# Attention values in two wide blocks with seven products, kept in the queries' place; row sums made for two pairs at a time, and early for the down products

## The chip, the core and the metric

The kernel runs on one core of a Trainium2 chip. The metric is the device time of one execution in microseconds. Each engine of the core has its own instruction stream: TensorE (PE in the profile; its weight loads are PEld) multiplies matrices into PSUM, VectorE (DVE) and ScalarE (ACT) compute elementwise, GpSimd (POOL) does little here, and SyncE (SP) issues the DMAs that bring data into SBUF.

## The reference

One layer of an encoder over 256 tokens with 2048 channels, in float32:

```
x = x + 1/2 * SwiGLU_1(RMSNorm(x))                      # hidden width 5632
P = RMSNorm(x) @ W_in                                    # pool group, and q, k, v, gates of a gated linear attention
x = x + concat(pool(P), gla(P)) @ W_out
x = x + CrossAttn(RMSNorm(x), RMSNorm(mem))              # 4 heads of 512, 256 memory tokens
x = x + 1/2 * SwiGLU_2(RMSNorm(x))
out = RMSNorm(x)

def mem_cross_attention(h, mem_h, w_q, w_kv, w_o):
    q = (h @ w_q).reshape(b, s, XATTN_HEADS, XATTN_HEAD_DIM)
    kv = (mem_h @ w_kv).reshape(b, mem_h.shape[1], 2, XATTN_HEADS, XATTN_HEAD_DIM)
    k, v = kv[:, :, 0], kv[:, :, 1]
    logits = jnp.einsum('bshd,bmhd->bhsm', q, k).astype(jnp.float32) * (XATTN_HEAD_DIM ** -0.5)
    p = jax.nn.softmax(logits, axis=-1).astype(v.dtype)
    o = jnp.einsum('bhsm,bmhd->bshd', p, v).reshape(b, s, D_MODEL)
    return o @ w_o
```

## The kernel before

**Split products.** Every float32 factor is split into a high part, rounded to a format that TensorE takes at full rate (`hi`), and the rest (`lo`). A product is three matmuls: hi·hi, hi·lo and lo·hi. Activations lie transposed in two arrays of 16 tiles of 128 channels (k-tiles): `xs`, the normed input, and `ys`, what the next projection reads (the hidden values, the mixer's output, or the queries and then the attention's output). Weights come from memory in **units** of 1 MB (`raw`). For each unit ACT makes the high half (`wh`) and DVE the low half (`wl`). `Stream` lists units and operations; an operation given with a number waits for so many units. Splits are recorded two units ahead (`AHEAD`), loads four further ahead (`RAW`).

**Blocks.** `block_a` puts the weights on TensorE's fixed side and yields channels by tokens (queries, keys). `block_b` yields tokens by 512 columns (values, 4 units of 4 k-tiles). `block_t` yields tokens by 1024 columns (8 units of a pair of k-tiles, 24 matmuls each). `block_s` is `block_t` with some units by Strassen's scheme in Winograd's form: the pair of k-tiles, the two token tiles and the two column halves make a 2 by 2 by 2 product, done in seven products of three matmuls (21) in place of eight (24). The units of this kind are called **pairs** here, by their place among the 8. They cost elementwise work: `split_seven` splits three quarters of the weights alone (`xh`, `xl`), makes four sums in `raw`, and splits these into `wh`, `wl`; `part_sums` makes the sums of the activations (`T`, then `xe` or `ye`, and one quarter back into `xs` or `ys`); `combine` and `joined_to` put the parts together. `block_s` keeps four PSUM tiles, which is all there are: two with the plain results, two with the parts.

**Stages.** FFN 1 runs over 11 blocks of 512 hidden columns in parts of 4, 4 and 3 (`FF_PARTS`): per two blocks a gate block of 1024 columns and an up block, then transposes (`turn`) into `ys`; after each part the down product adds to x (`into_x`). Pairs in gate and up are 1, 2, 4 and 5 of 8, in down 2 and 5 (of 8) or 2 and 4 (of 6), in the two output projections 3 and 5. The very first gate block of FFN 1 is plain. Then come the mixer, its output projection, the cross attention, its output projection, and FFN 2. The first gate block of FFN 2 has three pairs (2, 4, 5), whose row sums are made within the folding of x (`fold`, `folded`). In the attention come four blocks of queries, and then for each head 512 columns of keys, logits and softmax, 512 columns of values (`block_b`), and the weighted values. The row factor of the norm of x multiplies the queries as they are evicted (`joined(..., rows["R"])`); it is spread over the partitions by two matmuls with `ones` (`spread_norm`).

**The order.** No engine's order is written out by hand. `Recorder` notes each instruction as a task with its dependencies and a cost from `cost`; `Plan.schedule` places the tasks engine by engine (`forward`), by the latest start that a backward pass gave (`late`), six rounds, and keeps the best. In `pick`, an engine whose most urgent task isn't ready may first run another one that ends before that task's start. TensorE takes the ready task that was recorded first.

Of the kernel before, what the change touches and what calls it, by code (L numbers as in the profile page):

```python
# [17 lines left out]
P = 128  # L18
# [62 lines left out]
def cost(engine, name, args, kw, writes, reads):  # L81
# [123 lines left out]
class Plan:  # L205
# [150 lines left out]
    def schedule(self):  # L356
# [93 lines left out]
    def forward(self):  # L450
# [30 lines left out]
        def pick(e):  # L481
# [37 lines left out]
    WAIT = 0.2  # L519
    MARGIN = 1.01  # L520
# [42 lines left out]
def build(ctx, tc, I, out):  # L563
# [12 lines left out]
    def open_scope(name):  # L576
        def f():
            scope["now"] = plan.open(name)
        return f
# [22 lines left out]
    def ctile():  # L602
        return local([P, 2, S], F32, tag="c", name=uid("c"), bufs=2)
# [25 lines left out]
    ones = tile_of(const, [P, P], F32, "ones", "ones")  # L629
    nc.vector.memset(ones, 1.0)  # L630
    invc = ctl("invc", [P, PAD])
    for t in range(PAD):
        nc.gpsimd.memset(invc[:, t : t + 1], 1.0 / (t + 1))
    gains = ctl("gains", [P, G_END])
    Rcol = ctl("Rcol", [P, 2])
    Rm = ctl("Rm", [P, 2])
# [42 lines left out]
    def spread(ps, t, d):  # L679

        nc.tensor.matmul(ps[:, t * P : (t + 1) * P], ones, d, start=True, stop=True)
# [22 lines left out]
    diag, rows = {}, {}  # L704
# [97 lines left out]
    def part_sums(act, ext, g):  # L802


        t = tile_of(tmp, [P, NB], F32, tag="j", name=uid("T"), bufs=1)
        a = t.rearrange("p (k s) -> p k s", k=2)
        e = t.rearrange("p (n s) -> p n s", n=4)
        nc.vector.tensor_tensor(
            out=a, in0=f32(act[:, 2 * g : 2 * g + 2, 0, :]), in1=f32(act[:, 2 * g : 2 * g + 2, 1, :]),
            op=ALU.add,  # L810
        )
        nc.vector.tensor_tensor(out=e[:, 1], in0=e[:, 3], in1=e[:, 1], op=ALU.subtract)
        for n, by in ((0, 1), (3, 0)):
            nc.vector.scalar_tensor_tensor(
                out=e[:, n], in0=e[:, by], scalar=-1.0, in1=e[:, n], op0=ALU.mult, op1=ALU.subtract
            )
# [23 lines left out]
    def seven(banks, act, ext, g, first, last, begins, weights):  # L840
# [5 lines left out]
        s2, n1, n4 = ([ext[g][:, p, n] for p in range(2)] for n in range(3))  # L846
# [17 lines left out]
    def block_s(srcs, act, ext, pairs, evict, spare=None, joins=(1, 0), delays=(0, 0)):  # L864
# [3 lines left out]
        held, n = {}, len(srcs)  # L868
        plain = min(set(range(n)) - set(pairs))
# [19 lines left out]
        def unit_s(g):  # L889
            def fn(weights):  # L890
                open_banks(True)
                seven(held["banks"], act, ext, g, g == pairs[0], g == pairs[-1], begins, weights)
            return fn

        def unit_p(g):
            def fn(wh, wl):
                open_banks(False)
                wh, wl = (w.rearrange("p (k j n) -> p k j n", j=2, n=NB) for w in (wh, wl))
                for j in (1, 0):
                    for h in range(2):  # L900
                        for kk in range(2):
                            products(held["ps"][j][:, h, :], act, 2 * g + kk, h, wh[:, kk, j],
                                     wl[:, kk, j], begins(BANKS[j, h]), g == n - 1 and kk == 1)
# [16 lines left out]
        for g, src in enumerate(srcs):  # L920
            if g in pairs:
                st.unit(src, unit_s(g), split_seven)
                if g == pairs[-1]:
                    st.op(combine)
            else:
                st.unit(src, unit_p(g))
# [67 lines left out]
    def gain_columns(names, queue):  # L994
        t = rows["gain"] = local([P, P], F32, tag="gain", name=uid("gain"))
# [85 lines left out]
    def fold(c, gain, then=None):  # L1081
# [10 lines left out]
        if then:  # L1092
            then(c)
# [4 lines left out]
    def into_x(w, act, scale, gain=None, k0=0, nk=KT, spread_too=True, src=None, pairs=(), made=2,  # L1098
               then=None):


        ext = {}
        if pairs:
            st.op(lambda: sums_of(act, ext, pairs, "ye"), made)
        for b in range(2):
# [3 lines left out]
            if pairs:  # L1109
                block_s(srcs, act, ext, pairs, lambda *x, evict=evict: evict(1, *x), add, joins=(0, 1))  # L1110
            else:
                block_t(srcs, act, lambda *x, evict=evict: evict(1, *x))
            if gain is not None:
                for j in range(2):
                    st.op(lambda c=2 * b + j: fold(c, gain, then), 1)
# [4 lines left out]

    FF_PARTS = ((0, 4), (4, 4), (8, 3))
# [11 lines left out]
    xe = {}  # L1133

    def gate_sums(pairs):

        for g in pairs:
            if not len(xe) % (len(PAIRS) + 1):
                xe.clear()
                xe["all"] = local([P, len(PAIRS), 2, 3, P], F32R, tag="xe", name=uid("xe"))  # L1140
            xe[g] = xe["all"][:, PAIRS.index(g)]
            part_sums(xs, xe[g], g)

    def folded(c):
        gate_sums([g for g in PAIRS[1:] if g // 2 == c])

    def ffn(wg, wu, wd, down, first=()):
        gate = {}

        def joined_to(ev):  # L1150
            def evict(j, ps, e, op):
                nc.vector.tensor_tensor(out=e, in0=ps, in1=e, op=op)
                ev(j, e)
            return evict
# [644 lines left out]
```

## Time and profile before

| | us |
|---|---|
| median of 3 runs (lowest to highest) | 2108.31 (2106.38 to 2108.83) |
| the profiled execution, in all | 2110.4 |
| its span, first to last instruction | 2108.6 |
| TensorE busy | 2083.8 |
| VectorE busy | 1790.3 |
| ScalarE busy | 1133.0 |

All instructions that go through the recorder have one line, L548, so groups are told apart by the names of their tiles, out<-in: `pt`, `pa`, `pb`, `pe` are PSUM tiles of the blocks, `raw` is a loaded unit, `wh`, `wl`, `xh`, `xl` are its halves, `sg` and `x` are working tiles of tokens by columns, `px` the transposes of x, `ph` those of the hidden values. The stages lie, by the timeline of TensorE, at: FFN 1 from 7 to 714 us, mixer to 919, its output projection to 1005, queries to 1123, keys and values to 1300, the attention's output projection to 1389, FFN 2 to the end.

### The profile page before, as it was taken

How to read it: one execution, taken by the hardware profiler on the slowest of the kernel's cores; microseconds unless marked ns; L12 is line 12 of the kernel's file. 1: busy time of each engine (PE TensorE's matmuls, PEld its weight loads, DVE VectorE, ACT ScalarE, POOL GpSimd, SP SyncE). 2: the span in 40 equal slices, each digit the busy share in tenths (PEclk: the TensorE clock that was granted, in tenths of full speed). 3: DMA queues.
4: the chain of work that ended last, by engine and by line, in shares of the span. 5: the costliest groups of instructions: out<-in, count | busy, mean ns of one | idle time of the engine just before them, and what ended most of it. 6: DMA issues, size and time to landing. Idle time of an engine off the chain costs nothing.

```text
span 2108.6 us, 24534 instructions
## 1 busy us (share of the span) xinstructions
PE 2083.8 (99%) x9861; PEld 1734.4 (82%) x9861; DVE 1790.3 (85%) x1709; ACT 1133.0 (54%) x1046; POOL 15.8 (1%) x41
## 2 busy tenths in 40 slices
PE   9999999999999999999999999999999999999998
PEld 7888878888888888888888888877888888888886
DVE  7999899998999877688665545989998999989974
ACT  7665455654555555355644444557564555544643
POOL 0000000000000000000000000000000000000001
PEclk9999999999999999999999999999999999999999
DMA  8556656566656656457655555755567555776572
GB/s 293 187 189 227 244 201 217 179 240 232 226 180 239 224 181 198 145 181 262 246 181 165 170 168 160 239 180 208 192 208 262 208 199 180 239 240 219 192 268 99
DMA packets 143321, 435.95 MB, mean 207 GB/s; under 512 B 9828, under 2 KB 13000, under 8 KB 142824
## 3 DMA queue, kind: packets, MB, share of 16 engines
q1 hardware_dynamic: 143176, 434.38, 60.1%
q8 instruction: 77, 1.26, 0.2%
q14 instruction: 36, 0.29, 0.0%
q10 hardware_dynamic: 32, 0.01, 0.0%
HBM read 417.58 MB, written 16.78 MB: 206 GB/s over the span
## 4 chain that ended last, share of the span: by engine, by line
PE 64%; DVE 21%; ACT 6%; issue 5%; DMA 4%; SPq 0%; ACTq 0%; DVEq 0%
PE pt L548 37%; PE pa L548 15%; DVE wl L548 8%; PE pb L548 6%; DVE raw L548 5%; DVE xl L548 3%; ACT wh L548 3%; PE pe L548 3%; DMA raw<-in_ffn_w_gate 2%; DVE sg L548 2%; DMA raw<-in_ffn_w_up 2%; ACT sg L548 2%; DVE x L548 1%; PE ph L548 1%; PE pv L548 1%
## 5 line engine op out<-in xcount | busy, mean ns | idle before, releaser
L548 ACT CAST wh<-raw 128x2048 fp32r<-128x2048 f32 (+2 forms) x383 | 719.0, 1886 | 650.2 <-DVE raw L548 277.9
L548 DVE TENSOR_TENSOR wl<-raw,wh 128x2048 fp32r<-128x2048 f32 (+2 forms) x382 | 856.9, 2260 | 193.3 <-ACT wh L548 191.6
L548 PE MATMUL pt<-wh,xs 128*128 128x512 f32 x1820 | 596.3, 392 | 1.9 <-ACT xs L548 0.8
L548 PE MATMUL pt<-wh,ys 128*128 128x512 f32 x1392 | 441.1, 390 | 0.0
L548 PEld LDWEIGHTS pt<-wh,xs 128*128 128x128 f32 x1820 | 342.5, 188 | 74.7 <-ACT wh L548 2.5
L548 PE MATMUL pt<-wl,xs 128*128 128x512 f32 x910 | 357.9, 394 | 7.4 <-DVE wl L548 7.0
L548 PE MATMUL pa<-xs,wh 128*128 128x512 f32 x912 | 320.1, 398 | 0.0
L548 DVE TENSOR_TENSOR raw<-raw 128x512 f32<-128x512 f32 x444 | 306.7, 691 | 12.2
L548 PEld LDWEIGHTS pt<-wh,ys 128*128 128x128 f32 x1392 | 261.3, 188 | 54.1
L548 PE MATMUL pt<-wl,ys 128*128 128x512 f32 x696 | 271.1, 390 | 0.0
L548 PE MATMUL pa<-xs,wl 128*128 128x256 f32 x896 | 248.8, 280 | 0.0
L548 PEld LDWEIGHTS pt<-wl,xs 128*128 128x128 f32 x910 | 171.3, 188 | 53.1 <-DVE wl L548 18.6
L548 DVE TENSOR_TENSOR xl<-raw,xh 128x1536 fp32r<-128x1536 f32 x111 | 194.0, 1752 | 15.9 <-ACT xh L548 15.9
L548 ACT CAST xh<-raw 128x1536 fp32r<-128x1536 f32 x111 | 164.4, 1482 | 75.0 <-DMA raw<-in_ffn_w_gate 26.2
L548 PEld LDWEIGHTS pa<-xs,wh 128*128 128x128 f32 x912 | 170.9, 188 | 39.6 <-issue 0.7
L548 PEld LDWEIGHTS pa<-xs,wl 128*128 128x128 f32 x896 | 169.3, 189 | 1.1
L548 PEld LDWEIGHTS pt<-wl,ys 128*128 128x128 f32 x696 | 130.7, 188 | 26.8 <-DVE wl L548 0.2
L548 DVE TENSOR_TENSOR sg<-pt,sg 128x1024 f32<-128x1024 f32 (+1 forms) x147 | 140.9, 966 | 7.8 <-ACT sg L548 6.7
L548 PE MATMUL pt<-wh,xe 128*128 128x512 f32 x332 | 125.0, 393 | 0.0
L548 PE MATMUL pb<-wh,xs 128*128 128x512 f32 x384 | 122.0, 392 | 0.0
L548 PE MATMUL pt<-xh,xs 128*128 128x512 f32 x332 | 119.4, 390 | 0.3 <-DVE x L548 0.3
L548 PEld LDWEIGHTS pb<-wh,xs 128*128 128x128 f32 x384 | 72.1, 188 | 15.2 <-issue 0.2
(179 smaller groups left out, 1801.2 us busy)
## 6 DMA issues: line engine op xcount, KB each, us to landing
raw<-in_ffn_w_down SPq DMA_DIRECT2D x88, 1024.0 KB, 5.6
raw<-in_ffn_w_up SPq DMA_DIRECT2D x80, 1024.0 KB, 5.2
raw<-in_ffn_w_gate SPq DMA_DIRECT2D x77, 1024.0 KB, 5.4
raw<-in_w_in SPq DMA_DIRECT2D x32, 1024.0 KB, 5.3
raw<-in_xattn_w_kv SPq DMA_DIRECT2D x32, 1024.0 KB, 5.3
raw<-in_w_out SPq DMA_DIRECT2D x16, 1024.0 KB, 5.6
raw<-in_xattn_w_q SPq DMA_DIRECT2D x16, 1024.0 KB, 5.3
raw<-in_xattn_w_o SPq DMA_DIRECT2D x16, 1024.0 KB, 5.5
```

Source lines behind the costliest of these rows:

```text
L548: return f(*(real(a) for a in args), **{k: real(a) for k, a in kw.items()})
```

## The change

- **Values.** For two heads at a time come the key block of the one with its logits and probabilities, the key block of the other with its own, and then one `block_s` of 1024 value columns for both, with pairs 2, 4 and 6 (`V_PAIRS`). The row sums of the memory's `xs` are kept apart from it (`xx`, four of them), as the keys of the next heads read `xs` again. V is written over the queries of its two heads in `ys`. In this scope `xh` and `xl` have one buffer in place of two.
- **Row factor of the queries.** It goes into the scale and the bias of the softmax's exponential (`sR`, `nR`). The spreading ahead of the queries is left out.
- **FFN 2's first gate block** is plain, as FFN 1's, and the row sums of all four pairs are made after six units of it (`gate_sums`).
- **Row sums** are made for two pairs at a time. Down products take the pairs 1 and 3 in the order `DOWN_ORDER`, three plain units first, and their sums are recorded behind the turning of the first two blocks.
- **Planner.** In `pick` the other task may now end as late as 1 us before the urgent one's latest start (`SLACK`). The cost of a matmul is 0.2278 in place of 0.2284.
- **Constants.** `ones` and `invc` are made in the mixer's scope, and the gains share a tile with `ye`.

```diff
-        busy = 0.2284 if n > 256 else 0.118 if n > 128 else 0.109
+        busy = 0.2278 if n > 256 else 0.118 if n > 128 else 0.109
...
+        self.span = 1.003 * sum(t.busy for t in self.tasks if t.engine == "tensor")
         for _ in range(self.ROUNDS):
             out, end = self.forward()
+            self.span = max(end)
...
             if u.start > soon:
-                fit = [t for t in q if t.start <= soon and soon + t.busy <= u.start]
+                by = max(u.start, u.late + self.span - self.SLACK)
+                fit = [t for t in q if t.start <= soon and soon + t.busy <= by]
...
-    def part_sums(act, ext, g):
-        t = tile_of(tmp, [P, NB], F32, tag="j", name=uid("T"), bufs=1)
-        a = t.rearrange("p (k s) -> p k s", k=2)
-        e = t.rearrange("p (n s) -> p n s", n=4)
+    def part_sums(act, ext, pairs):
+        n = len(pairs)
+        gs = slice(pairs[0], pairs[-1] + 1, pairs[-1] - pairs[0] or 1)
+        act = act.rearrange("p (g k) a s -> p g k a s", k=2)
+        t = tile_of(tmp, [P, 2 * NB], F32, tag="j", name=uid("T"), bufs=1)[:, : n * NB]
+        a = t.rearrange("p (g k s) -> p g k s", g=n, k=2)
+        e = t.rearrange("p (g n s) -> p g n s", g=n, n=4)
...
-        nc.vector.tensor_tensor(out=e[:, 2], in0=e[:, 2], in1=e[:, 0], op=ALU.add)
-        split(act[:, 2 * g, 0, P:], act[:, 2 * g, 1, P:], e[:, 3])
-        split(ext[:, 0], ext[:, 1], e[:, 0:3])
+        nc.vector.tensor_tensor(out=e[:, :, 2], in0=e[:, :, 2], in1=e[:, :, 0], op=ALU.add)
+        n = ext.shape[3]
+        if n < 4:
+            split(act[:, gs, 0, 0, P:], act[:, gs, 0, 1, P:], e[:, :, 3])
+        split(ext[:, :, 0], ext[:, :, 1], e[:, :, 0:n])
...
-        alone = [local([P, 3 * NB], F32R, tag=n, name=f"{n}{u}", bufs=2) for n in ("xh", "xl")]
+        alone = [local([P, 3 * NB], F32R, tag=n, name=f"{n}{u}", bufs=scope["now"]["alone"])
+                 for n in ("xh", "xl")]
...
-    DOWN_PAIRS = {16: (2, 5), 12: (2, 4)}
+    DOWN_PAIRS = (1, 3)
+    DOWN_ORDER = {16: (0, 2, 4, 1, 5, 3, 6, 7), 12: (0, 2, 1, 4, 3, 5)}
     OUT_PAIRS = (3, 5)
+    W_OUT_PAIRS = (3, 5)
+    V_PAIRS = (2, 4, 6)
     def sums_of(act, ext, pairs, tag):
         t = local([P, len(pairs), 2, 3, P], F32R, tag=tag, name=uid(tag))
+        for i in range(0, len(pairs), 2):
+            part_sums(act, t[:, i : i + 2], pairs[i : i + 2])
         for i, g in enumerate(pairs):
             ext[g] = t[:, i]
-            part_sums(act, ext[g], g)
...
+                if not b and (lo + n < FF // NB or down is down_first):
+                    st.op(lambda: sums_of(ys, ye, DOWN_PAIRS, "ye"), wait)
...
+    def mem_sums(g):
+        if not xx:
+            xx["all"] = local([P, len(V_PAIRS), 2, 4, P], F32R, tag="xx", name=uid("xx"))
+        i = V_PAIRS.index(g)
+        xx[g] = xx["all"][:, i]
+        part_sums(xs, xx["all"][:, i : i + 1], (g,))
+
+    def x_factors():
+        nc.vector.tensor_scalar_mul(xt("nR", [P, 2]), Rcol, -(XHD ** -0.5))
+        nc.vector.tensor_scalar_mul(xt("sR", [P, 2]), Rcol, XHD ** -0.5)
...
-    st.op(open_scope("s_x"), 2)
-    st.op(row_factors, 2)
-    st.op(spread_norm, 3)
+    st.op(open_scope("s_x", 1, 3), 2)
+    st.op(x_factors, 2)
...
-    def ev_V(ps):
-        V = xt("V", [P, 2, 2, XHD], F32R, tag="kv", bufs=2)
-        split(V[:, :, 0, :], V[:, :, 1, :], ps)
+    def ev_V(b):
+        def evict(j, e):
+            k = 4 * (2 * b + j)
+            hi, lo = (ys[:, k : k + 4, a, :].rearrange("q (p m) c -> q p m c", m=2) for a in range(2))
+            split(hi, lo, e.rearrange("q m (p c) -> q p m c", p=2))
+        return evict
...
-    for h in range(H):
-        block_a(wblock(w_kv, h * NB), xs, ev_K)
+    for b in range(2):
+        h = 2 * b
+        block_a(wblock(w_kv, h * NB), xs, ev_K(h))
+        if not b:
+            for i, g in enumerate(V_PAIRS):
+                st.op(lambda g=g: mem_sums(g), 1 + i)
         st.op(lambda h=h: logits(h), 2)
         st.op(lambda h=h: probs(h), 3)
-        block_b(wblock(w_kv, D + h * NB), xs, ev_V)
-        st.op(lambda h=h: values(h), 1)
+        block_a(wblock(w_kv, (h + 1) * NB), xs, ev_K(h + 1))
+        st.op(lambda h=h: logits(h + 1), 1)
+        st.op(lambda h=h: probs(h + 1), 2)
+        block_s(wwide(w_kv, D + h * NB), xs, xx, V_PAIRS, joined_to(ev_V(b)))
+        for j in (1, 0):
+            st.op(lambda h=h, j=j: values(h + j), 1)
...
-    into_x(w_o, ys, 1.0, G_FFN2, spread_too=False, pairs=OUT_PAIRS, made=1, then=folded)
+    into_x(w_o, ys, 1.0, G_FFN2, spread_too=False, pairs=OUT_PAIRS, made=1)
...
-    st.op(lambda: gate_sums(PAIRS[:1]), PAIRS[0] + 1)
-    ffn(I["ffn2_w_gate"][0], I["ffn2_w_up"][0], I["ffn2_w_down"][0], down_last, PAIRS[1:])
+    st.op(gate_sums, PAIRS[-1] + 1)
+    ffn(I["ffn2_w_gate"][0], I["ffn2_w_up"][0], I["ffn2_w_down"][0], down_last)
```

More of the change, by code (lines that the diff above doesn't have):

```diff
@@ L574, in build, with open_scope @@
     scope = {}
-    def open_scope(name):
+    def open_scope(name, alone=2, c=2):
         def f():
             scope["now"] = plan.open(name)
+            scope["now"].update(alone=alone, c=c)
         return f
@@ L602, in ctile @@
     def ctile():
-        return local([P, 2, S], F32, tag="c", name=uid("c"), bufs=2)
+        return local([P, 2, S], F32, tag="c", name=uid("c"), bufs=scope["now"]["c"])
     def ttile():
@@ L679, in spread @@
     def spread(ps, t, d):
-        nc.tensor.matmul(ps[:, t * P : (t + 1) * P], ones, d, start=True, stop=True)
+        nc.tensor.matmul(ps[:, t * P : (t + 1) * P], mix["ones"], d, start=True, stop=True)
     def split_scaled(dst, kt, src, scale):
@@ L702, in row_squares @@
             nc.scalar.activation(j, src[h], AF.Square, accum_out=ss[:, h, c : c + 1])
-    diag, rows = {}, {}
+    diag, rows, mix = {}, {}, {}
     def finish_norm(n, spread_too=True):
@@ L862, in seven, with block_s @@
                 )
-    def block_s(srcs, act, ext, pairs, evict, spare=None, joins=(1, 0), delays=(0, 0)):
-        held, n = {}, len(srcs)
-        plain = min(set(range(n)) - set(pairs))
+    def block_s(srcs, act, ext, pairs, evict, spare=None, joins=(1, 0), delays=(0, 0), order=None):
+        held = {}
+        order = order or range(len(srcs))
+        lone = [g for g in order if g in pairs]
         def open_banks(parts):
@@ L891, in fn @@
                 open_banks(True)
-                seven(held["banks"], act, ext, g, g == pairs[0], g == pairs[-1], begins, weights)
+                seven(held["banks"], act, ext, g, "P2" not in fresh, g == lone[-1], begins, weights)
             return fn
@@ L1096, in fold, with into_x @@
             nc.scalar.activation(q, x[:, h], AF.Square, accum_out=ss[:, h, c : c + 1])
[L1098 to L1103, printed above, removed]
+    def into_x(w, act, scale, gain=None, k0=0, nk=KT, spread_too=True, src=None, pairs=(), made=2, order=None,
+               ext=None):
+        if pairs and ext is None:
+            ext = {}
             st.op(lambda: sums_of(act, ext, pairs, "ye"), made)
@@ L1109, in into_x @@
             if pairs:
-                block_s(srcs, act, ext, pairs, lambda *x, evict=evict: evict(1, *x), add, joins=(0, 1))
+                block_s(srcs, act, ext, pairs, lambda *x, evict=evict: evict(1, *x), add, joins=(0, 1),
+                        order=order)
             else:
@@ L1235, in mixer_constants @@
     def mixer_constants():
+        invc = mt("invc", [P, PAD])
+        for t in range(PAD):
+            nc.gpsimd.memset(invc[:, t : t + 1], 1.0 / (t + 1))
         keep = mt("keep", [P, S])
```

115 lines of the change are left out of this document (53 added, 62 removed).

## The prediction

> **What bounds the kernel now.** I read the page's busy shares first, then its chain of work that ended last, then TensorE's waits, then the busy times by stage.
>
> ```profile
> span 2108.6 us, 24534 instructions
> PE 2083.8 (99%) x9861; PEld 1734.4 (82%) x9861; DVE 1790.3 (85%) x1709; ACT 1133.0 (54%) x1046; POOL 15.8 (1%) x41
> PE 64%; DVE 21%; ACT 6%; issue 5%; DMA 4%; SPq 0%; ACTq 0%; DVEq 0%
> ```
>
> TensorE (PE) is busy for 99% of the span, so its number of matmuls sets most of the time. VectorE (DVE) carries 21% of the chain: in places it hands the weights over just in time, or late. All waits of TensorE by releaser, and below them those between 1380 and 1520 us:
>
> ```profile
> PE pt L548 <- DVE wl L548: 7.6, 14, 1.4
> PE px L548 <- DMA x<-in_x: 4.8, 2, 4.5
> ...
> PE pt L548 <- DVE wl L548: 3.9, 4, 1.4
> ```
>
> The columns are total us, times, longest. 4.8 us is the first load of x, which no change here touches. 7.6 us are waits for wl, the low half of a weight tile that DVE makes; 3.9 of them lie in one place. The view of windows says which: each row is a stretch, its length, then busy us (and instructions) of PE, PEld, DVE, ACT, POOL, then granted clock, DMA share and GB/s.
>
> ```profile
> 266.49:435.40 168.91, 167.28 (x738) 135.97 (x736) 165.29 (x136) 96.01 (x69) 0.00 (x0) 1.00 0.59 210
> 1122.91:1300.19 177.28, 177.28 (x953) 152.64 (x952) 93.15 (x83) 75.75 (x75) 0.00 (x0) 1.00 0.53 167
> 1389.18:1566.22 177.04, 171.63 (x756) 139.44 (x755) 170.49 (x168) 109.07 (x97) 0.00 (x0) 0.99 0.57 195
> 1652.34:1820.03 167.69, 166.80 (x738) 136.16 (x736) 163.79 (x135) 95.53 (x69) 0.00 (x0) 1.00 0.59 206
> ```
>
> The first, third and fourth rows are the same work: gate, up, gate, up of four blocks of 512 hidden columns; the third is the start of the second FFN. It takes 177.04 us where its twin takes 167.69. The second row is the K and V projections: PE never idle, DVE busy 53%.
>
> The price of a matmul, from the timeline:
>
> ```profile
> 1437.05 0.62 PE L548 MATMUL pt<-wh,xs 128*128 128x512 f32 x2
> 1437.50 0.39 PE L548 MATMUL pt<-wl,xs 128*128 128x512 f32 x1
> 1437.73 0.62 PE L548 MATMUL pt<-wh,xs 128*128 128x512 f32 x2
> ```
>
> Three matmuls of 512 columns start in 1437.73 − 1437.05 = 0.68 us, so one costs 0.227 us of path (its own 0.39 overlaps the next). And the price of a late weight, in the first gate block of the second FFN:
>
> ```profile
> 1403.06 0.47 PE L548 MATMUL pt<-wh,xs 128*128 128x512 f32 x1 [0.36 <-DVE xs L548]
> 1403.36 0.40 PE L548 MATMUL pt<-wh,xe 128*128 128x512 f32 x1
> 1405.16 0.79 PE L548 MATMUL pt<-wl,xs 128*128 128x512 f32 x1 [1.40 <-DVE wl L548]
> 1405.76 0.63 PE L548 MATMUL pt<-wh,xs 128*128 128x512 f32 x1
> 1406.18 0.63 PE L548 MATMUL pt<-wh,xe 128*128 128x512 f32 x1
> 1406.61 0.63 PE L548 MATMUL pt<-wl,xe 128*128 128x512 f32 x1
> ...
> 1408.32 0.52 PE L548 MATMUL pt<-xh,xs 128*128 128x512 f32 x1
> ```
>
> After idling 1.40 us PE starts a matmul every 0.43 us (1406.61 − 1406.18), half its rate: seven of them take 1408.32 − 1405.16 = 3.16 us, 3.16 − 7 × 0.227 = 1.6 us too long. A stall of over 1 us costs about twice itself.
>
> The Trainium skill, in "TensorE: Matmul & The Clock Gate", Part 1, says that the array falls to half clock after about 3.4 us of idleness. The trace has the half rate after 1.40 us, so the measurement decides. By the page's rule a short stall would cost itself alone, and the twin comparison below, made of measured lengths, would stand as it is.
>
> **The change part by part.** V: four blocks of 512 columns become two of 1024, in which the unit pairs 2, 4 and 6 of 8 take seven products in place of eight.
>
> ```profile
> L548 PE MATMUL pb<-wh,xs 128*128 128x512 f32 x256 | 81.4, 392 | 0.0
> L548 PE MATMUL pb<-wl,xs 128*128 128x512 f32 x128 | 49.9, 390 | 0.0
> ```
>
> Before, V has 256 + 128 = 384 matmuls. A plain unit is 2 k-tiles × 2 halves × 2 token tiles × 3 = 24; one of seven products is 7 × 3 = 21. Two blocks are 2 × (5 × 24 + 3 × 21) = 366: 18 fewer, 18 × 0.227 = **−4.1 us**. The matmuls of logits, probabilities and values keep their number and shapes.
>
> What V adds goes to DVE and ACT, priced by these groups (DVE's, then ACT's; us in total, then mean ns):
>
> ```profile
> L548 DVE TENSOR_TENSOR wl<-raw,wh 128x2048 fp32r<-128x2048 f32 x374 | 849.4, 2287 | 191.0 <-ACT wh L548 189.3 <-issue 0.2
> L548 DVE TENSOR_TENSOR raw<-raw 128x512 f32<-128x512 f32 x444 | 306.7, 691 | 12.2
> L548 DVE TENSOR_TENSOR xl<-raw,xh 128x1536 fp32r<-128x1536 f32 x111 | 194.0, 1752 | 15.9 <-ACT xh L548 15.9
> L548 DVE TENSOR_TENSOR sg<-pt,sg 128x1024 f32<-128x1024 f32 x77 | 92.7, 1220 | 0.8
> L548 DVE TENSOR_TENSOR sg<-pt,sg 128x512 f32<-128x512 f32 x70 | 48.1, 687 | 7.0 <-ACT sg L548 6.7
> L548 DVE TENSOR_TENSOR T<-T 128x128 f32<-128x128 f32 x44 | 12.7, 289 | 0.9
> L548 DVE SCALAR_TENSOR_TENSOR T<-T 128x128 f32<-128x128 f32 x44 | 12.7, 289 | 0.8
> L548 DVE TENSOR_TENSOR T<-ys 128x512 f32<-128x512 f32 x14 | 9.6, 686 | 0.0
> L548 DVE TENSOR_TENSOR t<-t,R 128x512 f32<-128x512 f32 x12 | 8.2, 688 | 0.2
> L548 DVE TENSOR_TENSOR ye<-T,ye 128x384 fp32r<-128x384 f32 x14 | 7.7, 552 | 0.0
> L548 DVE TENSOR_TENSOR V<-pb,V 128x1024 fp32r<-128x1024 f32 x4 | 4.9, 1226 | 8.6 <-ACT V L548 8.6
> L548 DVE TENSOR_TENSOR ys<-T,ys 128x128 fp32r<-128x128 f32 x14 | 4.0, 286 | 0.2 <-ACT ys L548 0.2
> L548 DVE TENSOR_TENSOR t<-t 128x256 f32<-128x256 f32 x4 | 1.7, 426 | 2.0 <-ACT t L548 2.0
> L548 ACT CAST wh<-raw 128x2048 fp32r<-128x2048 f32 x374 | 712.2, 1912 | 645.4 <-DVE raw L548 277.9 <-PE pt L548 128.7 <-issue 81.4
> L548 ACT CAST xh<-raw 128x1536 fp32r<-128x1536 f32 x111 | 164.4, 1482 | 75.0 <-DMA raw<-in_ffn_w_gate 26.2 <-DMA raw<-in_ffn_w_down 15.8 <-DMA raw<-in_ffn_w_up 14.6
> ```
>
> A seven-product weight adds 4 × 0.691 + 1.752 = 4.5 us of DVE and 1.5 of ACT; six of them 27 and 9. Row sums of one pair are 0.686 + 4 × 0.289 + 0.552 + 0.286 = 2.7; three make 8. Joining a block is 2 × 0.687 + 5 × 1.22 = 7.5 (combine, two joins, two splits); two make 15, less the 4 × 1.226 of the old eviction. DVE in the K/V stage goes from 93 to about 93 + 27 + 8 + 15 − 5 = 138 of 173 us, or 80%: still hidden behind PE. With that cover gone the 45 us would show. The row factor leaves the queries' eviction (8 × 0.688 = 5.5 us of DVE, hidden before) and enters the softmax's scale: nothing.
>
> Three waits are new. xh and xl have one buffer in this scope, so the split of the next seven-product weight waits until PE has read the last one; behind it on DVE stand the plain wl's, for which PE waits. All four PSUM tiles are taken by V's seven products, so the first of these waits until the softmax's transposes have left theirs; PE has matmuls on the other banks meanwhile. And V lands in the queries' place, so its split waits for the logits, which are issued one unit into the V block, seven units ahead of it. No row shows any of the three. At best they cost nothing (DVE has 35 us spare); the other end is the slow rival's 20. I take +0.5, near the lower end, since the row of this stage has PE without idleness and its engines half free.
>
> The second FFN's first gate block: 3 of its 8 units had seven products; now none has. That is 9 more matmuls, +2.0 us alone. In return 3 × 4.5 of DVE's splits and the block's joining go, and the row sums leave the folding of x and come after six units of that block, all four pairs in two goes. The first FFN already does it in this order. What the stage becomes I take from its twin: 12 matmuls more than the twin's (4 seven-product units × 3), and the 16 transposes of the folding.
>
> ```profile
> 1394.62 1.91 PE L548 MATMUL px<-ident,x 128*128 128x128 f32 x16
> 1396.29 0.47 PE L548 MATMUL pt<-wh,xs 128*128 128x512 f32 x1
> ```
>
> These take 1396.29 − 1394.62 = 1.67 us. So 167.69 + 12 × 0.227 + 1.67 = 172.1 us for 177.0: **−5.0 us**, the added matmuls included. By the other twin (168.91) it is −3.7; without any stall it would be 732 × 0.227 + 32 transposes at 1.67/16 = 169.5, or −7.5.
>
> The spreading of the row factor ahead of the queries goes:
>
> ```profile
> L548 PE MATMUL ps<-diag,ones x24: 270/275/276, 732.7 to 1023.8; 128*128 128x128 f32 x24
> ```
>
> Two of these, at the transposes' pitch (1.67/16 = 0.104): **−0.2 us**.
>
> Row sums by two pairs: 1.220 + 5 × 0.426 + about 0.96 (768 wide, between the 512 and the 1024 row) = 4.3 for two, against 5.4: 1.1 us less DVE, eleven times. Down products now begin with three plain units, and their sums come from pairs 1 and 3, which exist once the first half of the hidden columns is turned. The list planner may also let a short task run ahead of a due one that has slack. All this can only move the waits left outside the second FFN's start: 7.6 − 3.9 = 3.7 us for wl, so −3.7 at best, and as much worse if the new order is the less lucky. I take **−1.5**: DVE gets lighter in every stage, but stays near 98% busy in the twins (165.29 of 168.91). The constants ones and invc move into the mixer's scope: at the start they lie behind the 4.5 us wait for x, in the mixer POOL is idle. DMA: the same bytes, in rows twice as long for V, at a share of 0.53: nothing. SP's order otherwise stays.
>
> Sum: −4.1 + 0.5 − 5.0 − 0.2 − 1.5 = −10.3 us. The profiled execution took 2110.4 us in all (its span of 2108.6 and 1.8 around it), which would give 2100.1; against the median of the runs, 2108.31, it is **2098.0 us**.
>
> **The rivals.** *More goes.* The other stages lose all 3.7 us and the second FFN's start all its stalls: −4.1 − 7.5 − 0.2 − 3.7 = −15.5, 2092.8 us. For: lighter DVE everywhere. Against: the twins at 98%. Chance 0.16. *The stalls only move.* Four pairs of sums now fall into the turn from gate to up, and the stage keeps its stalls: −4.1 + 2.0 − 0.2 + 0.5 = −1.8, 2106.5 us. For: in the row above DVE is busy 170.49 of 177.04 us. Against: 18 us of that work go, and the first FFN has this order. Chance 0.12. *Slower: one buffer for xh and xl.* From release to high sums lies 1.482 + 1.752 + 4 × 0.691 + 1.912 = 7.9 us. PE needs them after 3 + 24 + 9 matmuls (8.2 us) at a block's second seven-product unit, after 12 + 24 + 9 (10.2) at its third. If two plain wl's (4.6 us) stand ahead on DVE, PE is 4.3 and 2.3 us late, 13.2 in two blocks; with 1.6 to 1.7 us of half rate after each of four stalls, 20 us: −10.3 + 20 = +9.7, 2118.0 us. It decides from 14.5 us, 3.6 a stall. For: a margin of 0.3 us. Against: DVE at 80%, and plain matmuls on other banks that can go first. Chance 0.06. That V isn't cut would show in the count alone; I see nothing for it.
>
> **How the numbers follow.** Forecast 0.66, the rivals 0.16, 0.12, 0.06. A measurement tells 0.2%, 4.2 us, from no change: faster means below 2104.1. Faster 0.66 + 0.16 = 0.82, same 0.12, slower 0.06. The low end is the first rival's 2092.8. The high end takes the worse of each bound, −4.1 + 0.5 − 3.7 − 0.2 + 3.7 = −3.8: 2104.5. Beyond lie the other two rivals and little else.
>
> **What would show it.** Right: no pb<-xs products of V; some 11 fewer matmuls; the stage after the attention's output near 172 us at clock 1.00; PE's wait for wl near 3; DVE near 80% in K/V with PE at its full length, 173 us. Wrong: gaps of PE in K/V after xh or wl, or a first up block of the second FFN that waits for xs or xe. A shift of several us in stages that the change leaves alone would mean that the planner's new order matters more than the matmuls.

## The result and the profile after

| | before | after |
|---|---|---|
| median of 4 runs, us (lowest to highest) | 2107.35 (2105.47 to 2108.83) | 2094.26 (2093.22 to 2098.17) |
| profiled execution, span | 2108.6 | 2093.1 |

The ratio is 0.9942, with a 95% interval of 0.9925 to 0.9959: 9 to 16 us faster, 13.1 by the medians. The forecast was −10.3. The profiled execution of the kernel before was a long one: 2110.4 us in all, 3.0 over its median, where that of the changed kernel took 2095.1, 0.8 over its own. So the spans differ by 15.5 us, 2.4 more than the medians.

The page of the changed kernel, the lines that answer to those shown first:

```profile
span 2093.1 us, 24446 instructions
PE 2075.1 (99%) x9848; PEld 1731.4 (83%) x9848; DVE 1800.9 (86%) x1660; ACT 1136.1 (54%) x1029; POOL 15.0 (1%) x42
PE 85%; DVE 9%; ACT 2%; issue 2%; DMA 2%; DVEq 0%; SPq 0%; ACTq 0%
```

TensorE has 13 records fewer and is busy 8.7 us less; the span fell by 15.5. So some 7 us came out of waits. The records that went are worth about 2.5 us (18 × 0.227 + 4 × 0.104 − 9 × 0.227); the rest of the busy time is records that took longer before, as those behind a late weight do. The chain agrees: VectorE's share fell from 21% to 9%, although VectorE does 10.6 us more work. Its work ends last less often. TensorE's waits by releaser (total us, times, longest), the changed kernel:

```profile
PE px L552 <- DMA x<-in_x: 4.4, 1, 4.4
PE pt L552 <- DVE wl L552: 3.3, 6, 1.3
PE pt L552 <- DVE x L552: 0.2, 1, 0.2
PE ph L552 <- DVE sg L552: 0.2, 1, 0.2
```

The wait for wl went from 7.6 us in 14 cases to 3.3 in 6. The windows of the changed kernel that answer to those of the forecast (length; busy PE, PEld, DVE, ACT, POOL; clock, DMA share, GB/s): FFN 1's second stage of gate and up, keys and values, FFN 2's first stage, FFN 2's second.

```profile
265.21:430.67 165.46, 165.46 (x737) 136.44 (x736) 161.76 (x134) 95.87 (x69) 0.00 (x0) 1.00 0.59 209
...
1117.90:1288.77 170.87, 170.87 (x914) 146.46 (x913) 121.90 (x113) 85.44 (x80) 0.00 (x0) 1.00 0.52 170
...
1380.67:1551.00 170.33, 170.27 (x766) 140.44 (x764) 153.30 (x140) 102.50 (x90) 0.00 (x0) 1.00 0.59 202
...
1637.82:1804.93 167.11, 166.31 (x737) 136.20 (x736) 161.41 (x134) 94.52 (x69) 0.00 (x0) 1.00 0.60 208
```

FFN 2's first stage went from 177.04 to 170.33 us and its clock from 0.99 to 1.00. TensorE is busy through all of keys and values, with VectorE at 71%. But FFN 1's second stage also lost 3.45 us (168.91 before), though the change leaves its matmuls as they are. To compare what has the same bounds in both kernels, the attention is taken whole, from the first matmul of the queries to the first of FFN 2. First before, then after:

```profile
1005.02:1389.18 384.16, 384.16 (x2058) 330.70 (x2056) 247.72 (x246) 191.60 (x225) 0.00 (x0) 1.00 0.59 192
```

```profile
1000.50:1380.67 380.17, 380.17 (x2035) 326.54 (x2034) 280.69 (x280) 201.91 (x231) 0.00 (x0) 1.00 0.59 194
```

So the 15.5 us of the span fall into three parts: attention −4.0, FFN 2's first stage −6.7, everything else −4.8. The last part is the one to explain, and it holds whatever was particular to the two executions that were profiled.

### The profile page after: what moved, and what is told of

Read it like the earlier page. It is cut to its first block, busy times and chain, and to the rows that moved or that the text cites. A ratio compares the mean times of both kernels' runs of the same rounds, so it can differ in the third digit from the quotient of the medians.

```text
span 2093.1 us, 24446 instructions
## 1 busy us (share of the span) xinstructions
PE 2075.1 (99%) x9848; PEld 1731.4 (83%) x9848; DVE 1800.9 (86%) x1660; ACT 1136.1 (54%) x1029; POOL 15.0 (1%) x42
## 4 chain that ended last, share of the span: by engine, by line
PE 85%; DVE 9%; ACT 2%; issue 2%; DMA 2%; DVEq 0%; SPq 0%; ACTq 0%
PE pt L552 61%; PE pa L552 15%; DVE wl L552 3%; PE pe L552 3%; PE pb L552 2%; DVE raw L552 2%; DVE xl L552 1%; DVE sg L552 1%; ACT wh L552 1%; DMA raw<-in_ffn_w_down 1%; PE ph L552 1%; PE px L552 1%; DVE x L552 1%; PE pl L552 1%; PE pv L552 1%
## 5 line engine op out<-in xcount | busy, mean ns | idle before, releaser
L552 DVE TENSOR_TENSOR wl<-raw,wh 128x2048 fp32r<-128x2048 f32 (+2 forms) x382 | 856.8, 2259 | 168.4 <-ACT wh L552 166.3
L552 PE MATMUL pt<-wh,xs 128*128 128x512 f32 x2028 | 657.1, 391 | 0.3 <-DVE x L552 0.2
L552 PEld LDWEIGHTS pt<-wh,xs 128*128 128x128 f32 x2028 | 380.9, 188 | 81.2 <-ACT wh L552 2.1
L552 PE MATMUL pt<-wl,xs 128*128 128x512 f32 x1014 | 395.4, 391 | 1.1 <-DVE wl L552 1.1
L552 DVE TENSOR_TENSOR raw<-raw 128x512 f32<-128x512 f32 x456 | 314.7, 690 | 12.0
L552 PEld LDWEIGHTS pt<-wl,xs 128*128 128x128 f32 x1014 | 190.5, 188 | 43.4 <-DVE wl L552 4.6
L552 DVE TENSOR_TENSOR xl<-raw,xh 128x1536 fp32r<-128x1536 f32 x114 | 199.1, 1752 | 18.8 <-ACT xh L552 18.8
L552 DVE TENSOR_TENSOR sg<-pt,sg 128x1024 f32<-128x1024 f32 (+1 forms) x152 | 146.7, 968 | 13.7 <-ACT sg L552 12.1
L552 PE MATMUL pt<-wh,xe 128*128 128x512 f32 x320 | 119.0, 390 | 0.0
L552 PEld LDWEIGHTS pt<-xh,xs 128*128 128x128 f32 x344 | 64.6, 188 | 13.4
L552 PEld LDWEIGHTS pt<-wh,xe 128*128 128x128 f32 x320 | 60.1, 188 | 12.7
```

The costliest lines, as they stand in the source:

```text
L552: return f(*(real(a) for a in args), **{k: real(a) for k, a in kw.items()})
```

## The experiments

All were timed beside the kernel before, five rounds each, on three chips: its median was 2107.21 us beside e1 to e4, 2106.06 beside e5 to e8 and 2107.82 beside e9 to e12. So kernels of different groups are better compared by their ratios than by their medians. Below, **gate and up** is the sum of the six gate and up stages (three in each FFN; the expectations call them five, but their 924.9 us is the sum of all six), **down** that of the five down products ahead of the last one, **attention** as above. Each is read from the starts of TensorE's matmuls in one profiled execution, from the first of a stage to the first of the next.

| kernel | gate and up | FFN 1's second | FFN 2's first | down | median | ratio to before (95%) |
|---|---|---|---|---|---|---|
| before | 939.5 | 168.9 | 177.0 | 411.1 | 2107.35 | |
| after | 924.9 | 165.5 | 170.3 | 413.6 | 2094.26 | 0.9942 (0.9925 to 0.9959) |
| e1_old_rule | 926.9 | 166.5 | 170.3 | 412.0 | 2093.59 | 0.9938 (0.9925 to 0.9950) |
| e2_rule_alone | 936.8 | 166.4 | 176.0 | 410.7 | 2109.28 | 1.0009 (1.0000 to 1.0018) |
| e3_first_gate_seven | 928.4 | 165.5 | 174.7 | 412.6 | 2097.39 | 0.9953 (0.9941 to 0.9966) |
| e4_old_values | 925.8 | 166.8 | 170.3 | 411.5 | 2098.48 | 0.9961 (0.9948 to 0.9973) |
| e5_one_pair | 925.0 | 166.0 | 170.3 | 412.0 | 2093.19 | 0.9938 (0.9925 to 0.9950) |
| e6_old_down | 925.8 | 166.3 | 170.3 | 417.7 | 2101.06 | 0.9972 (0.9962 to 0.9983) |
| e7_old_sums_and_down | 929.3 | 166.4 | 170.3 | 411.0 | 2096.46 | 0.9948 (0.9936 to 0.9961) |
| e8_plain_gate_alone | 929.7 | 166.5 | 169.6 | 410.7 | 2100.14 | 0.9971 (0.9960 to 0.9983) |
| e9_late_record | 925.1 | 165.5 | 170.3 | 411.7 | 2093.25 | 0.9939 (0.9926 to 0.9953) |
| e10_before_cost | 937.2 | 167.1 | 176.2 | 411.5 | 2107.72 | 1.0000 (0.9991 to 1.0009) |
| e11_after_cost | 926.5 | 166.2 | 170.2 | 411.7 | 2094.05 | 0.9936 (0.9924 to 0.9949) |
| e12_one_pair_old_rule | 926.3 | 166.9 | 170.6 | 411.9 | 2094.54 | 0.9941 (0.9928 to 0.9953) |

### The values (e4)

The changed kernel with the old values: `block_b` in four blocks of 512 columns, V in a tile of its own, and keys and values head by head. Of the edit, the lines of the blocks:

```diff
-        block_s(wwide(w_kv, D + h * NB), xs, xx, V_PAIRS, joined_to(ev_V(b)))
-        for j in (1, 0):
-            st.op(lambda h=h, j=j: values(h + j), 1)
+        block_b(wblock(w_kv, D + h * NB), xs, ev_V)
+        st.op(lambda h=h: values(h), 1)
```

> The changed kernel with the values as before: four blocks of 512 columns without seven products, a V tile of their own, keys and values head by head. 18 matmuls more. Theory D (TensorE bounds this stage and the added VectorE work is hidden): keys, values and the attention's output projection together take 4.0 to 4.4 us more than the 262.8 us of the changed kernel, and the whole 4 us more. Rival (part of the 18 matmuls is given back as waits or in the stages behind): the whole moves by under 2 us.

The attention stage of this kernel:

```profile
1001.23:1385.31 384.08, 384.02 (x2053) 330.05 (x2052) 238.95 (x222) 190.37 (x220) 0.00 (x0) 1.00 0.59 192
```

384.08 − 380.17 = 3.9 us for 18 matmuls at 0.227 (4.1), and the whole is 4.2 us over the changed kernel (4.0 by the ratios). Against this kernel the new values cost VectorE 280.69 − 238.95 = 41.7 us in the stage, and TensorE is busy for every us of it in the changed kernel. The work is hidden, as the forecast had it.

### FFN 2's first gate block (e8 and e3)

Once by itself in the kernel before (e8), once taken back in the changed kernel (e3). The edit of e8:

```diff
-    into_x(w_o, ys, 1.0, G_FFN2, spread_too=False, pairs=OUT_PAIRS, made=1, then=folded)
+    into_x(w_o, ys, 1.0, G_FFN2, spread_too=False, pairs=OUT_PAIRS, made=1)
...
-    st.op(lambda: gate_sums(PAIRS[:1]), PAIRS[0] + 1)
-    ffn(I["ffn2_w_gate"][0], I["ffn2_w_up"][0], I["ffn2_w_down"][0], down_last, PAIRS[1:])
+    st.op(lambda: gate_sums(PAIRS), PAIRS[-1] + 1)
+    ffn(I["ffn2_w_gate"][0], I["ffn2_w_up"][0], I["ffn2_w_down"][0], down_last)
```

> The kernel before with one edit: FFN 2's first gate block is plain, and the row sums of its four pairs come after six units of it, one pair at a time. Nine matmuls more, 2.0 us. Theory C: its stage falls from 177.05 to 170 to 172 us, the granted clock there is 1.00, the whole is 5 to 7 us faster than before. Rival (the stalls move into the first up block): 174 to 179 us, the whole within 2 us of before.

> The changed kernel with three units of seven products in FFN 2's first gate block and their row sums made one pair at a time within the folding of x, as before the change. Nine matmuls fewer, 2.0 us. Theory C (this block's extra VectorE work caused the stalls at FFN 2's start): its first stage goes from 170.3 to 176 to 178 us with waits for wl and a granted clock under 1.00, the whole about 6.5 us over the changed kernel. Rival (the planner's new rule alone fills them): the stage falls to 168 to 169.5 us and the whole is 1 to 2 us under the changed kernel.

FFN 2's first stage in e8, then in e3:

```profile
1385.54:1555.18 169.64, 169.64 (x766) 140.65 (x764) 157.39 (x156) 103.99 (x94) 0.00 (x0) 1.00 0.60 204
```

```profile
1380.23:1554.97 174.74, 171.35 (x756) 139.42 (x755) 167.86 (x167) 107.67 (x97) 0.00 (x0) 0.99 0.58 197
```

With nine matmuls *more*, the stage of e8 is 7.4 us shorter than before, and TensorE is never idle in it. In e3 the waits and the clock of 0.99 are back, with VectorE busy 96% (167.86 of 174.74). That is what the theory of this block says, though e3's stage is 174.7 and not 176 or more, and its whole 3.1 us over the changed kernel (2.3 by the ratios), not 6.5. The rival (the planner's rule fills them) falls. Three units of seven products in the place where VectorE has also x to fold and the sums to make cost more than the 2.0 us they save. The edit moves the products and the sums together, so which of the two makes the stalls isn't separated.

### The planner's rule and the plan itself (e1, e2, e10, e11)

e1 takes the new rule out of the changed kernel (the edit shown); e2 puts it, with the matmul cost of 0.2278, into the kernel before:

```diff
-                by = max(u.start, u.late + self.span - self.SLACK)
-                fit = [t for t in q if t.start <= soon and soon + t.busy <= by]
+                fit = [t for t in q if t.start <= soon and soon + t.busy <= u.start]
```

> The changed kernel with the planner's old rule for filling (a task may go ahead of an urgent one only if it ends before that one's start). All else as changed. Theory A, the rule brought the 3 to 5 us that the gate and up stages lost beyond the forecast: the second gate and up stage of FFN 1 (165.46 us in the changed kernel, 168.91 before) goes back to 168 to 169.5 us, TensorE waits for wl in it again, and the whole is about 5 us over the changed kernel, 8 us under the kernel before. Theory B, the lighter row sums and their place brought them: the stage stays at 165 to 166.5 us and the whole within 1.5 us of the changed kernel, 12 to 13 us under the kernel before.

> The kernel before with the planner's new rule, its span and the matmul cost of 0.2278, and nothing else. Theory A (the rule brings the gain of the gate and up stages): FFN 1's second stage falls from 168.91 to about 165.5 us, the others by 0.5 to 2 us each, the whole is 5 to 8 us faster. Theory B (the row sums): all stages within 1 us of before, the whole within 2 us.

e10 and e11 do nothing but plan anew: 0.2278 for a matmul in the kernel before, 0.2284 in the changed one.

```diff
-        busy = 0.2284 if n > 256 else 0.118 if n > 128 else 0.109
+        busy = 0.2278 if n > 256 else 0.118 if n > 128 else 0.109
```

> The kernel before with the planner's matmul cost 0.2278 instead of 0.2284: the same instructions in a new plan. Theory G (part of the gain beyond the forecast is that FFN 1's second stage, 168.91 us, was unlucky in the plan before): that stage falls to 166 to 167 us, FFN 2's first stays at 175 to 178, the other stages move by up to 1 us either way, the whole within 3 us of before. Rival: the stage stays at 168.5 us or more, and only the edits of the change shorten it.

> The changed kernel with the matmul cost 0.2284 of before: the same instructions in a new plan. It measures what a plan without a reason is worth: within 2 us of the changed kernel, FFN 2's first stage at 170 to 171 us, keys and values with no wait of TensorE. A larger move would mean that single differences of 1 to 3 us between the other runs tell nothing.

Without the rule the changed kernel is as fast (0.9938 beside 0.9942), and with it the kernel before is no faster (1.0009). The rule does nothing that can be measured; theory A of these runs falls. What a new plan does was worth knowing. FFN 1's second stage in e10:

```profile
265.52:432.65 167.13, 166.49 (x738) 136.26 (x736) 162.69 (x135) 95.90 (x69) 0.00 (x0) 1.00 0.58 207
```

The same instructions, 1.8 us less than before; and in no kernel but the one before is this stage over 167.2 us. It looks like an unlucky plan before, as theory G has it, but the traces say otherwise. Up to 437 us VectorE runs the same instructions in the same order in both. In the kernel before it is about 1.0 us later than in e10 up to 233 us, and 3.3 us later at 260. Between the two, ACT waits for one load of a gate weight, in the kernel before and then in e10:

```profile
252.28 1.48 ACT L548 CAST xh<-raw 128x1536 fp32r<-128x1536 f32 x1 [4.76 <-DMA raw<-in_ffn_w_gate]
```

```profile
248.97 1.48 ACT L548 CAST xh<-raw 128x1536 fp32r<-128x1536 f32 x1 [2.42 <-DMA raw<-in_ffn_w_gate]
```

This load landed 7.8 us after its issue (at 244.47) in the kernel before and 5.4 us (at 243.51) in e10; VectorE was later by as much behind it, and TensorE waits for VectorE. So most of what the change "gained" in this stage is a load that was 2.3 us late in the one execution that was profiled; why it was late, one execution can't show. The medians agree: e10 is level with before (1.0000). With one profile of each kernel, what a new plan does can't be told from what an execution does. The two together moved the sum of the gate and up stages by 1.6 us (e11 beside the changed kernel) to 2.3 (e10 beside before); a new plan moved the medians by under 0.5.

### Row sums and down products (e5, e6, e7, e9, e12)

e5 makes the sums one pair at a time; e6 puts back the down products' pairs, order and late sums; e7 does both; e9 keeps pairs and order and only records the sums late; e12 is e5 with the old rule.

The first edit is that of e5, e7 and e12, the second that of e6 and e7. e9 has the removal of the early sums and of `ext=ye` alone.

```diff
-        for i in range(0, len(pairs), 2):
-            part_sums(act, t[:, i : i + 2], pairs[i : i + 2])
+        for i in range(len(pairs)):
+            part_sums(act, t[:, i : i + 1], pairs[i : i + 1])
```

```diff
-    DOWN_PAIRS = (1, 3)
-    DOWN_ORDER = {16: (0, 2, 4, 1, 5, 3, 6, 7), 12: (0, 2, 1, 4, 3, 5)}
+    DOWN_PAIRS = {16: (2, 5), 12: (2, 4)}
...
-                if not b and (lo + n < FF // NB or down is down_first):
-                    st.op(lambda: sums_of(ys, ye, DOWN_PAIRS, "ye"), wait)
...
-               pairs=DOWN_PAIRS, order=DOWN_ORDER[nk], ext=ye)
+               pairs=DOWN_PAIRS[nk])
...
```

> The changed kernel with the row sums made for one pair at a time (22 + 3 calls instead of 11 + 3), in the same places. About 1.1 us more VectorE work per two pairs. Theory E (the lighter sums took the waits out of the gate and up stages): FFN 1's second stage goes from 165.5 to 167 us or more, FFN's five gate and up stages together 3 to 5 us longer, the whole 3 to 5 us over the changed kernel. Rival F (place and order of the down sums) and rival G (any new plan puts the waits elsewhere): these stages within 1.5 us of the changed kernel in sum, the whole within 1.5 us.

> The changed kernel with the down products as before: pairs 2 and 5 (2 and 4 of six), natural order, row sums after two units of the product. Theory F (sums recorded early and three plain units first took the waits away): the gate and up stages are 3 to 5 us longer in sum, above all FFN 1's second, 165.5 to 168 us or more, and the whole 2 to 4 us over the changed kernel; the 0.7 to 1.0 us that the two down stages of FFN 2 lost (86.1 to 86.8 and 87.1) come back. Rivals E and G: gate and up stages within 1.5 us in sum, the whole level or 1 to 2 us lower.

> The changed kernel with both of these undone: sums one pair at a time and the down products as before; the values, FFN 2's plain first gate block, the planner's rule and the constants stay. If E and F together make the gain of the gate and up stages: these stages 5 to 6 us longer in sum, the whole 5 us over the changed kernel (about 2099 us). If neither does (G, the plan as a whole, or the other parts): within 2 us of the changed kernel.

> The changed kernel with the down sums recorded two units into the down product, as before, while pairs 1 and 3 and the order with three plain units first stay. If the order alone gives room (the first unit of seven products comes one unit later), the five gate and up stages stay at 925 to 927 us in sum (924.9 in the changed kernel), the down stages at 411 to 414 us, the whole within 1.5 us of the changed kernel. If recording early is what counts, the down stages wait for ye, 3 to 7 us longer in sum, and the whole is 3 to 7 us over the changed kernel.

> The changed kernel with the row sums one pair at a time and the planner's old rule: what is left are the values, FFN 2's plain gate block and the new down products. If these three carry the whole gain: within 1.5 us of the changed kernel, 12 to 14 us under the kernel before. If the rule and the two-pair sums help together though neither does alone: 3 us or more over the changed kernel.

**Two pairs at a time: nothing, with the new order.** e5 is level with the changed kernel (0.9938, gate and up 925.0 for 924.9), though its VectorE has more to do (1807.7 us busy for 1800.9). **With the old order it harms.** e6 differs from e7 only in making two pairs at a time, and is 4.6 us slower: its gate and up stages are 3.5 us shorter, its down stages 6.7 longer. Neither case of its expectation came. TensorE's waits in e6, the first two rows, and the first down product, e6 and then e7:

```profile
PE pt L552 <- ACT ye L552: 5.1, 5, 1.4
PE px L552 <- DMA x<-in_x: 4.5, 2, 4.0
```

```profile
179.31:267.13 87.82, 86.41 (x389) 71.45 (x388) 77.98 (x65) 41.65 (x27) 0.00 (x0) 1.00 0.66 228
```

```profile
181.34:267.43 86.09, 86.09 (x390) 71.52 (x388) 77.91 (x71) 41.74 (x29) 0.00 (x0) 1.00 0.67 233
```

Five down products, five waits for ye, the high half of the sums: one in each. The timeline of e6 at the first one shows how (TensorE, then VectorE, then ACT):

```profile
193.34 0.39 PE L552 MATMUL pt<-wh,ys 128*128 128x512 f32 x1
195.14 0.50 PE L552 MATMUL pt<-xh,ye 128*128 128x512 f32 x1 [1.41 <-ACT ye L552]
195.48 0.39 PE L552 MATMUL pt<-xl,ye 128*128 128x512 f32 x1
```

```profile
190.62 1.23 DVE L552 TENSOR_TENSOR T<-ys 128x1024 f32<-128x1024 f32 x1
```

```profile
194.26 0.83 ACT L552 CAST ye<-T 128x768 fp32r<-128x768 f32 x1
```

A sum of two pairs can't start before the later pair is there. In e6 this is pair 5, whose hidden values are turned only behind the start of the down product (at 179.3): the sums start at 190.62, and pair 2 needs them in the third unit. In e7, the first pair's own sums start 9 us ahead of the product (at 172.3, for 181.3). With pairs 1 and 3 both are there early, and two at a time costs nothing.

**The order: 2 to 3 us.** e5 and e7 both make sums singly and differ in the down products alone: 2093.19 and 2096.46, 3.3 us by the medians, 2.1 by the ratios (0.9938 and 0.9948, whose intervals overlap); in the profiles gate and up are 4.3 shorter, down 1.0 longer. That is under the 5 us that e7 was expected to lose if sums and order counted together. One pair of runs wouldn't carry this, but the other kernels agree. Gate and up without FFN 2's first stage, by the table, are 753.7 to 756.6 us in the eight kernels with the new order, and 759.0 to 762.5 in the five with the old order and single sums. e6 is the exception: with the old order and sums by two pairs it has 755.5. So the new order isn't the only way to short gate and up stages; beside sums by two pairs, what it saves is the waits for ye. Whether e6's lighter sums shorten these stages, or its waits in the down products give VectorE time, no run separates.

e9 has the new order with sums recorded late, and is level with the changed kernel. So it is the pairs and their order that count, and not when the sums are recorded: the planner starts them 9 us ahead of the down product either way (at 1542.0 in the changed kernel, for a product that starts at 1551.0; at 1540.7 for 1549.7 in e9). That the later first unit of seven products is what frees VectorE at the end of the up blocks is my reading; no run shows it by itself.

e12, without the two-pair sums and the rule, is level with the changed kernel (0.9941). **The values, the plain gate block and the order of the down products leave nothing that can be measured to the other edits:** 4.0 (e4), about 6 (e8: 2106.06 before on the same chip, less 2100.14) and 2 to 3 make 12 to 13, beside 13.1 measured. Each part is known to a us or two, so the sum fits better than it had to. None of the runs is clearly faster than the changed kernel; e5, e9 and e1 are level with it.

## Why the forecast held, point by point

**TensorE's count.** Right. 18 + 4 fewer and 9 more make the 13 records missing on the page. The 4 are a mis-sizing: each of the two spreading products is two records.

```profile
L552 PE MATMUL ps<-diag,ones x20: 270/275/275, 727.6 to 897.3; 128*128 128x128 f32 x20
```

24 before and 20 after, so the term was −0.4 and not −0.2. I had taken the count from the code instead of from the row.

**Values, −4.1 + 0.5, and −0.2 for the spreading.** Right: the attention gave 3.99 us for a forecast of 3.8. None of the three new waits is seen, so the slow rival, xh and xl with one buffer, fell, and the 0.5 can't be told from noise. VectorE's added work was forecast at 45 us, and is 42 in e4's comparison; its share in keys and values became 71%, not the 80% of the forecast.

**FFN 2's first stage, −5.0.** Right in kind, 1.7 us short: −6.7, and −7.4 in e8. The twin by which it was sized, 167.69 us, had stalls of its own (0.9 us of idle TensorE), and the other, 168.91, has the late load. The lower bound from counted matmuls, 169.5 us, was the better guide: the stage took 170.33 and 169.64. The rival in which the stalls move into the first up block fell with TensorE's 170.27 busy us of 170.33.

**Everything else, −1.5, bounded at ±3.7.** In the profiles this is −4.8, beyond the bound, in spite of 2.5 us that the down products lost. But 2.4 us of it belong to the profiled executions (15.5 by the spans, 13.1 by the medians), as the load that was 2.3 us late shows. About −2.4 is left: inside the bound, the term 0.9 too small. The sign set for the planner, a shift of several us in stages that the change leaves alone, did appear in FFN 1's second stage, and was mostly this load. Two things were wrong all the same. I took it for planner's noise and lighter sums, when the pairs and order of the down products were a cause with 2 to 3 us of its own; the sums by two pairs, which I did count on, gave nothing beside it. And the bound was the total of TensorE's *idle* time for wl. A stall costs more than its idle time, as the timeline of the changed kernel shows in the fourth down product:

```profile
1581.32 0.39 PE L552 MATMUL pt<-wh,ys 128*128 128x512 f32 x1
1582.15 0.50 PE L552 MATMUL pt<-wl,ys 128*128 128x512 f32 x1 [0.44 <-DVE wl L552]
1582.49 0.39 PE L552 MATMUL pt<-wh,ys 128*128 128x512 f32 x1
```

From the first start to the third are 1.17 us where two matmuls take 0.45: 0.7 us lost for 0.44 of idleness. The 0.39 us of a matmul overlap the next by 0.16, which a stall uses up before it shows as idle, and the matmul behind it takes 0.34 to the next start. FFN 1's second stage before had 1.63 us of idle TensorE and was 3.45 us longer than after. Stage lengths over counted matmuls give a wider bound: 720 × 0.227 + 16 × 0.104 = 165.1 us leaves 3.8 and 2.6 us in the two twins alone, more than the 3.7 taken for all stages.

**The constants' move** was costed at nothing. The mixer, before and then after, took 0.6 us more:

```profile
714.24:918.89 204.65, 204.65 (x1149) 176.71 (x1148) 147.16 (x200) 103.05 (x117) 5.26 (x12) 1.00 0.56 180
```

```profile
709.12:914.39 205.27, 205.27 (x1149) 176.89 (x1148) 148.25 (x200) 103.11 (x117) 4.99 (x28) 1.00 0.56 179
```

It has the same number of matmuls and no idle TensorE in either. The plan doesn't make the difference: the mixer takes 204.6 to 204.7 us in the four kernels with the constants at the start (before, e2, e8, e10), and 205.2 to 205.3 in the ten with them in the mixer's scope. How they cost 0.6 us isn't shown.

**The price of a stall** was put too high, on the other hand: "over 1 us costs about twice itself" came from one place. In e6, above, 1.41 us of idleness are followed by matmuls at 0.34 and then the full rate: from 193.34 to 195.48 are 2.14 us where two matmuls take 0.45, 1.7 us lost, 1.2 times the idle time. So the 6 to 7 us of half rate within the slow rival's 20 us weren't bound to come; the last section shows when the half rate came.

## What to carry to other kernels

In a kernel bound by TensorE, count the matmuls of each stage, multiply by the measured pitch, and compare with the stage's length; the rest is what an edit there can return, and idle time understates it. A trick that saves matmuls by elementwise work pays where the elementwise engine has room (the values, VectorE at 71%) and cost more than it saved in one block where that engine was nearly full (FFN 2's first gate block: its stage 7.4 us shorter by giving up a saving of 2.0). When a planner orders everything, time a plan that was changed for no reason before a difference of 1 to 2 us in one stage is given a cause, and compare the profiled execution with the median: here one late load made 2.3 us of such a difference.

## What the runs showed of the hardware

The half rate of TensorE doesn't follow the length of one gap. In the kernel before, a gap of 1.40 us was followed by seven matmuls at 0.43 us; in e6 a gap of 1.41 us was followed by the full rate of 0.23 within two. The place doesn't decide it either: in e2 the gaps of 0.39 and 1.40 us stand at the same matmuls as those of 0.36 and 1.40 in the kernel before, and the full rate follows.

The clock's own record in the traces tells more. Leaving out the end of a kernel, where TensorE runs out of work, it falls four times, once each in before, e2, e3 and e10, always to 0.50 for 3.41 us. Each fall lies a whole number of such stretches after the clock first rose (in the kernel before at 9.12 us; 409 stretches of 3.413 us later is 1405.17). Cut at these points, two stretches each of before, e2 at the same gaps, and e2 at its fall, then the one of e6's gap (length; busy PE; the granted clock is the third number from the end):

```profile
1401.76:1405.17 3.41, 1.65 (x8) 0.74 (x6) 3.41 (x5) 1.64 (x1) 0.00 (x0) 1.00 0.00 0
1405.17:1408.58 3.41, 3.41 (x8) 2.73 (x9) 3.38 (x3) 0.00 (x0) 0.00 (x0) 0.50 0.65 193
...
1399.24:1402.65 3.41, 1.82 (x7) 1.23 (x8) 3.41 (x3) 0.54 (x1) 0.00 (x0) 1.00 0.07 7
1402.65:1406.07 3.42, 3.42 (x17) 2.81 (x16) 3.35 (x5) 1.23 (x1) 0.00 (x0) 1.00 0.93 323
1457.27:1460.68 3.41, 1.53 (x7) 1.04 (x6) 3.41 (x2) 3.38 (x4) 0.00 (x0) 1.00 0.18 20
1460.68:1464.09 3.41, 3.41 (x9) 2.65 (x9) 3.14 (x2) 2.98 (x4) 0.00 (x0) 0.50 0.89 321
...
193.47:196.88 3.41, 2.00 (x10) 1.43 (x9) 3.41 (x4) 2.02 (x3) 0.00 (x0) 1.00 0.21 55
```

In the stretches ahead of the four falls TensorE is busy for 1.53 to 1.73 us of 3.41 (1.60 in e3, 1.73 in e10), and behind stretches with 1.82 and 2.00 the full clock stays. So in these traces it is the idle time within a fixed stretch that goes with the half clock, and the same gaps can fall on either side of a cut. One stretch at the very end of e1, busy for 1.54 us, has no fall behind it; no run was made to test the reading.
